# Reordering the first layer's GLU, query/key and gate groups, the pace of the convolution's taps, and the split of q and k, in a hybrid conformer and attention trunk

## The chip, the cores and the metric

The kernel runs on one core of a Trainium2 chip. The metric is device time in microseconds (us) of one execution; "the time before" is the median of three runs. In the profile PE is TensorE (PEld its weight loads), DVE is VectorE, ACT is ScalarE, POOL is GpSimd and SP is SyncE, whose queue issues most of the DMAs.

## What is computed

Two layers over 256 latent tokens (a grid of 4 rows of 64) and 256 context tokens, 1024 channels wide. The second layer (the last) carries only the latent stream and takes keys and values of the context. Of the reference, per layer, cut to the part around the change:

```python
h = modulate(rmsnorm(x, norm1_g[l]), sh1, sc1)      # and hc for the context
p = h @ w_in[l]        # columns: a, g (512 each), q, k, v (512 each), gates (2 x 1024)
...
u = a * sigmoid(g)                                   # "gated channels" (GLU)
u = dwconv1d(u, dw, dw_b)                            # 31 taps along the tokens
y_conv = silu(layernorm(u, ln_g, ln_b)) @ w_o
...
q = rope_2d(q, pos_row, pos_col); k = rope_2d(k, pos_row, pos_col)
y_attn = neighbourhood_attention(q, k, v, k_ctx, v_ctx, rpb) @ w_na_out
yc_attn = context_attention(q_c, k_c, v_c) @ w_na_out      # first layer only
...
x = x + g1 * ((sigmoid(gate_c) * y_conv + sigmoid(gate_a) * y_attn) @ w_out[l])
```

A gated FFN with a convolution of width 3 follows in each layer. The modulation (`sh1`, `sc1`, `g1` and three more of 1024 channels each) is a product of the conditioning vectors with `w_ada`. Everything is float32.

## The kernel before

Channels lie on the 128 partitions, tokens in the free dimension: columns 0 to 255 latent, 256 to 511 context, so an operation over both streams is 512 wide. The kernel is written with a tile framework: the Python code traces instructions in an order, and the framework's planner then puts the instructions of each engine in order, by the traced order among those that its cost model holds to be ready. It may bring a later instruction forward. `tc.issue_after(ins)` adds an edge by which the instructions inside it stand behind `ins` on the engine of `ins`. Each engine executes its list in order.

**A matmul in three parts.** Every product is taken with both operands split in a high part and a rest (`hi`, `lo`): `mm3` (L196 to L199) issues hi x hi, hi x lo and lo x hi. A weight unit of 128 x 1024 comes by `raw_unit` through SP (four buffers), ScalarE casts it (L167 or L216), and the rest is made on VectorE (L168) or, for units in `ADDED`, on ScalarE and a GpSimd DMA that adds (L217, L218). `group` (L201) runs the 24 matmuls of one projection tile; over both streams it calls `slot()` after the twelfth and after the last.

**Slots.** `slot()` (L92) advances every side task by one step. In the first layer's attention stage there are two: `conv_run` (L677), which adds `rate[0]` to a debt and traces as many convolution taps as are due, and `att.run()` (L452), which steps the attention.

**Taps.** `glu(j, ...)` (L687) makes the gated channels `u` of channel block j (0 to 3) from two projection groups (`glu_groups`, L701), with a tanh on ScalarE and a product on VectorE (L693), and appends 31 taps of block j to a list of 124 in all. Each tap is one VectorE instruction, 128 x 512 (L671 for the first of a block, L673 for others). `conv_tap` puts a tap behind the instruction in `after[0]`, which is the latest score (L516, L530).

**Pairs.** Attention works on four pairs of heads. `qk(j)` (L843) projects q and k of pair j (a group each, Q and K), loads the pair's bias, turns the latent part by the rotary tables (L859 to L869: product, shuffle, product, sum on VectorE) and splits the result and the context's part, which is not turned, into `hi` (L881, ScalarE) and `lo` (L882, VectorE). The context's part is read straight from PSUM. For k the latent part is written twice, as `[0, KL)` (the right end of each grid row) and `[KX, KN)` (the left end), with the context between them. The first of a pair's two score products reads context and left end, the second right end and context.

**Attention.** `step` (L457) does at most one round of work per slot, and only when enough slots (2 to 4) lie behind the last round: it turns the probabilities of the round before (`turn`, L544, transposes on TensorE and copies on ScalarE L564 or L567), multiplies older ones by the values (L578, L587), and issues the next score product (`products`, L495) with its softmax (`scores`, L507: L516 on VectorE, L519 exponential and L522 scaling on ScalarE, L521 reciprocal on VectorE). Rounds are "LAT" (a pair's latent queries) and "CTX" (the context's, for two pairs together). `ahead(j)` forces the rounds of pair j and of those before it. PSUM has four banks for projections (`main`), two (`sc`) and one (`pt`) for scores and transposes, and one (`po`).

**Order in the first layer.** After the values (`keep_v`, L719, with 16 small DMAs through SP) come pair 0, GLU 1, pair 1, GLU 2, pair 2, GLU 3, pair 3; GLU 0 was made before. Then up to five gate groups (`gate`, L708) while attention is busy. `rate[0]` is 2 up to pair 1, then 3. Next a second memory pool is opened in place of attention's tiles: in it `ada_dots` (L289) loads further modulation weights (`own`) and multiplies them on VectorE (L304), and `layer_norm` (L938) traces the taps that are left, five a slot, sums the blocks (L949 to L951) and takes that sum to TensorE (L955) five slots later. The remaining gates, the branch products (L993, L998 to L1001) and the output projection follow. The second layer has an order of its own (GLU 2, values, pair 0, GLU 3, then a gate ahead of each further pair), 256 columns for q and 512 for k.

## Time and profile before

| what | value |
|---|---|
| median of three runs | 1056.28 us |
| lowest, highest | 1054.83, 1057.64 us |
| the profiled execution | 1054.58 us |
| its span, first to last instruction | 1052.8 us |
| granted TensorE clock, mean | 0.997 |
| matmuls | 6886 |
| HBM read | 187.63 MB |

The span is what the trace covers; the profiled execution's own time includes some 1.8 us around it. Rows of a timeline give start, duration, engine, line, operation, output and inputs, and in brackets the engine's idle time before the instruction with what ended it. Rows of stretches give the stretch, its length, and then for each engine the busy time with the number of instructions; after these the granted clock, the DMA share and GB/s. A matmul's end is modelled, and matmuls overlap, so the distance from one start to the next tells what one costs.

### The profile page before, as it was taken

The numbers are of one execution on the slowest core, as the hardware profiler recorded it, in microseconds if no ns is written. First come the engines' busy times: TensorE is split into PE (matmuls) and PEld (weight loads), VectorE is DVE, ScalarE is ACT, GpSimd is POOL, SyncE is SP. The second block draws the span as 40 slices with busy tenths as digits, with TensorE's granted clock in tenths as the row PEclk, the third lists the DMA queues.
The fourth block names the chain that finished last, engine by engine and source line by source line (L and its number), as shares of the span: only waits on it lengthen the run. The fifth ranks groups of instructions, "written<-read, shape, count | busy, mean of one in ns | idle before, by whom it ended". The sixth has DMA issues, their size and how long they took to land.

```text
span 1052.8 us, 17991 instructions
## 1 busy us (share of the span) xinstructions
PE 1032.4 (98%) x6886; PEld 932.9 (89%) x6886; DVE 893.2 (85%) x1608; ACT 565.6 (54%) x921; POOL 43.7 (4%) x59
## 2 busy tenths in 40 slices
PE   9999999999999999999999999999999999999997
PEld 7787788888889988888888889999889999999996
DVE  6568899999998787878788888799899988988883
ACT  4458768545434644444444223545777666766652
POOL 1111110011000000000000000000000000000000
PEclk9999999999999999999999999999999999999998
DMA  9989674888945345454545887556734485666781
GB/s 374 305 221 229 156 181 121 258 255 236 305 146 177 104 140 160 140 164 143 166 145 160 301 289 249 180 189 209 208 123 135 161 292 176 193 201 199 221 283 57
DMA packets 59511, 209.26 MB, mean 199 GB/s; under 512 B 7201, under 2 KB 7457, under 8 KB 59425
## 3 DMA queue, kind: packets, MB, share of 16 engines
q1 hardware_dynamic: 54384, 190.77, 55.3%
q0 software_dynamic: 4752, 17.30, 8.7%
q8 instruction: 54, 0.88, 0.3%
q14 instruction: 33, 0.26, 0.1%
q10 hardware_dynamic: 288, 0.04, 0.0%
HBM read 187.63 MB, written 1.05 MB: 179 GB/s over the span
## 4 chain that ended last, share of the span: by engine, by line
PE 68%; DVE 17%; ACT 5%; DMA 4%; issue 3%; SPq 1%; DVEq 0%; ACTq 0%
PE main L197 20%; PE main L198 20%; PE main L199 20%; DVE cb L673 6%; PE main L736 4%; DVE wlo L168 3%; DMA raw<-in_wall 2%; DVE t L304 2%; DMA own<-in_wada 1%; SPq L728 1%; PE sc L197 1%; PE sc L199 1%; PE sc L198 1%; DVE qk L882 1%; ACT pp L519 1%
## 5 line engine op out<-in xcount | busy, mean ns | idle before, releaser
L197 PE MATMUL main<-h,whi 128*128 128x256 f32 (+1 forms) x1328 | 433.1, 326 | 1.2 <-DVE qk L882 1.2
L198 PE MATMUL main<-h,whi 128*128 128x256 f32 (+1 forms) x1328 | 430.2, 324 | 0.9 <-DVE h L1001 0.7
L199 PE MATMUL main<-h,wlo 128*128 128x256 f32 (+1 forms) x1328 | 429.9, 324 | 1.2 <-DVE wlo L168 1.1
L167 ACT CAST whi<-raw 128x1024 fp32r<-128x1024 f32 (+1 forms) x211 | 218.3, 1039 | 234.8 <-PE main L198 173.6
L168 DVE TENSOR_TENSOR wlo<-raw,whi 128x1024 fp32r<-128x1024 f32 (+1 forms) x211 | 253.6, 1208 | 67.2 <-ACT whi L167 66.4
L197 PEld LDWEIGHTS main<-h,whi 128*128 128x128 f32 x1328 | 252.8, 190 | 22.0 <-issue 1.3
L199 PEld LDWEIGHTS main<-h,wlo 128*128 128x128 f32 x1328 | 252.5, 190 | 18.5 <-DVE wlo L168 1.8
L198 PEld LDWEIGHTS main<-h,whi 128*128 128x128 f32 x1328 | 252.7, 190 | 18.3 <-DVE h L1001 1.0
L304 DVE CUSTOM_DVE_ANT_0 t<-own,sb,par 128x1024 bf16<-128x1024 f32 x120 | 151.8, 1282 | 6.8 <-DMA own<-in_wada 6.8
L673 DVE SCALAR_TENSOR_TENSOR cb<-u,par,cb 128x512 f32<-128x512 f32 (+1 forms) x240 | 144.7, 620 | 2.8
L198 PE MATMUL main<-fl,whi 128*128 128x256 f32 (+1 forms) x396 | 122.8, 310 | 0.0
L197 PE MATMUL main<-fh,whi 128*128 128x256 f32 (+1 forms) x396 | 122.8, 310 | 0.0
L199 PE MATMUL main<-fh,wlo 128*128 128x256 f32 (+1 forms) x396 | 122.5, 310 | 0.0
L197 PEld LDWEIGHTS main<-fh,whi 128*128 128x128 f32 x396 | 75.6, 191 | 3.8 <-ACT fh L1095 0.2
L198 PEld LDWEIGHTS main<-fl,whi 128*128 128x128 f32 x396 | 75.6, 191 | 3.7 <-DVE fl L1096 0.2
L199 PEld LDWEIGHTS main<-fh,wlo 128*128 128x128 f32 x396 | 75.5, 191 | 3.6
L216 ACT CAST whi<-raw 128x1024 fp32r<-128x1024 f32 x33 | 34.6, 1049 | 36.0 <-PE main L198 30.5
L404 ACT ACTIVATE h<-t,mod 128x256 fp32r<-128x256 f32 x56 | 25.2, 503 | 34.8 <-DVE t L403 34.3
L218 POOL DMA_DIRECT2D wlo<-raw x33 | 28.9, 877 | 258.9 <-ACT wlo L217 107.6
L736 PE MATMUL main<-whi,h 128*128 128x512 f32 x128 | 38.5, 386 | 0.2
L1105 ACT ACTIVATE t<-t 128x512 f32<-128x512 f32 x22 | 13.9, 632 | 41.3 <-DVE t L1074 41.3
L217 ACT ACTIVATE wlo<-whi 128x1024 fp32r<-128x1024 f32 x33 | 35.0, 1061 | 0.5
(214 smaller groups left out, 1268.8 us busy)
## 6 DMA issues: line engine op xcount, KB each, us to landing
raw<-in_wall SPq DMA_DIRECT2D x240, 512.0 KB, 4.3
own<-in_wada SPq DMA_DIRECT2D x72, 512.0 KB, 4.7
wlo<-raw POOLq DMA_DIRECT2D x33, 512.0 KB, 5.4
raw<-in_wada SPq DMA_DIRECT2D x16, 512.0 KB, 5.8
bias<-in_bias_t SPq DMA_DIRECT2D x8, 520.0 KB, 5.3
row<-in_wada SPq DMA_DIRECT2D x8, 512.0 KB, 5.1
sb<-in_crow SPq DMA_DIRECT2D x5, 512.0 KB, 4.8
x<-in_xt SPq DMA_DIRECT2D x4, 512.0 KB, 5.1
```

Source lines behind the costliest of these rows:

```text
L167: act.copy(hi[:, c], r[:, c])
L168: dve.tensor_tensor(lo[:, c], r[:, c], hi[:, c].bitcast(F32), ALU.subtract)
L197: pe.matmul(ps, w[0], order(xh), start=start, stop=False)
L198: pe.matmul(ps, w[0], order(xl), start=False, stop=False)
L199: pe.matmul(ps, w[1], order(xh), start=False, stop=stop)
L216: act.copy(hi, r)
L217: act.mul(lo, hi.bitcast(F32), -1.0)
L218: pool.dma_start(lo, r, accum_op=ALU.add)
L304: dve.tensor_tensor_reduce(tmp().bitcast(BF16), r, v, 1.0, pr(l, BADA + n, 1), ALU.mult, ALU.add, mods[l][:, n, s : s + 1])
L404: high = act.activation(hi[:, c], y[:, c], AF.Identity, bias=b)
L673: dve.scalar_tensor_tensor(cb[j], src, w, cb[j], ALU.mult, ALU.add)
L736: mm = pe.matmul(pv[t], h1[n == 1][k][:, c], runs(w[n == 2][:, b]), start=k + n == 0, stop=k == KD - 1 and n == 2)
```

## The change

In the first layer GLU 1 is traced before pair 0, and GLU j + 1 before pair j for j = 1 and 2; pair 3 is preceded by gate 0 in place of a GLU group. `glu_groups` asks `ahead` for one pair less, so the rounds that it forces stay at the same pair. The convolution's rate is 3 taps a slot, but for the first group of GLU 2 and of GLU 3 (2 taps a slot). Up to eight gate groups, instead of five, may be traced while attention is busy. For pairs 1 to 3 of the first layer `after[0]` is set to the last split of q, and then to that of k, so that taps traced later stand behind it on VectorE. In both layers the split of the context's part is traced before the second product of the rotation instead of after its sum, and the two ends of k change places: the left end first.

```diff
@@ glu_groups
             def glu_groups(j):
+                if not last and j > 1:
+                    rate[0] = 2.0
                 pa = in_group(T_GLU + 2 * (j - 1), ALL)
+                if not last and j > 1:
+                    rate[0] = 3.0
                 pg = in_group(T_GLU + 2 * (j - 1) + 1, ALL)
-                copied = None if last else att.ahead(j - 2)
+                copied = None if last else att.ahead(j - 3)
...
                 conv = conv_run()
-                rate[0] = 3 if last else 2.0
+                rate[0] = 3.0
                 add_side(conv)
 
+                def parts(f, d, src, sc, view=lambda a: a):
+                    hi, lo = (view(f[:, a, d]) for a in range(2))
+                    act.activation(hi, src, AF.Identity, scale=sc)
+                    return dve.scalar_tensor_tensor(lo, src, sc, hi.bitcast(F32), ALU.mult, ALU.subtract)
+
                 def qk(j):
 
                     att.ahead(j - 2)
+                    if not last:
+                        rate[0] = 3.0
...
                         dve.stream_shuffle(part(r2[:, LAT]), lat, SWAP16)
+                        f = eb.tile([P, 2, KN if what else w], F32R, tag="qk"[what], bufs=2, name=nm("qk"))
+                        if ctx_ is not None:
+                            parts(f, KCTX if what else CTX, ctx_, sc)
                         dve.tensor_tensor(r2[:, LAT], r2[:, LAT], rope[:, 1, :], ALU.mult)
...
                         if what == 0:
-                            to = [([f[:, a, LAT] for a in range(2)], rq[:, LAT])]
-                            if T > S:
-                                to.append(([f[:, a, CTX] for a in range(2)], ctx_))
+                            end = parts(f, LAT, rq[:, LAT], sc)
                         else:
                             rv_ = r1[:, LAT].rearrange("p (r c) -> p r c", r=ROWS)
-                            to = [([f[:, a, KCTX] for a in range(2)], ctx_)]
-                            for d, c in ((slice(0, KL), slice(GW - TC, GW)), (slice(KX, KN), slice(0, TC))):
-                                to.append(([f[:, a, d].rearrange("p (c r) -> p r c", r=ROWS) for a in range(2)], rv_[:, :, c]))
-                        for (hi, lo), src in to:
-                            act.activation(hi, src, AF.Identity, scale=sc)
-                            end = dve.scalar_tensor_tensor(lo, src, sc, hi.bitcast(F32), ALU.mult, ALU.subtract)
+                            for d, c in ((slice(KX, KN), slice(0, TC)), (slice(0, KL), slice(GW - TC, GW))):
+                                end = parts(f, d, rv_[:, :, c], sc, lambda a: a.rearrange("p (c r) -> p r c", r=ROWS))
+                        if not last and j:
+                            after[0] = end
                         both.append(f)
                     att.pair(j, *both, bt, end)
+                    rate[0] = 3.0
 
                 if l == 0:
                     for t in range(4):
                         keep_v(t, pv[t])
+                    rate[0] = 3.0
+                    glu_groups(1)
                     qk(0)
                     arun = att.run()
                     add_side(arun)
-                    for j in range(1, 4):
-                        glu_groups(j)
+                    for j in range(1, 3):
+                        glu_groups(j + 1)
                         qk(j)
-                        rate[0] = 3
...
                 if last:
                     add_side(arun)
-                    for j in range(1, 4):
+                for j in range(1 if last else 3, 4):
+                    if True:
                         gate(ea, n)
                         n += 1
                         qk(j)
-                while att.busy() and n < (14 if last else 5):
+                while att.busy() and n < (14 if last else 8):
                     gate(ea, n)
                     n += 1
```

More of the change, by code (lines that the diff above doesn't have):

```diff
@@ L869, in qk @@
                             dve.tensor_tensor(r1[:, LAT], r1[:, LAT], r2[:, LAT], ALU.add)
-                        f = eb.tile([P, 2, KN if what else w], F32R, tag="qk"[what], bufs=2, name=nm("qk"))
                         if what == 0:
-                            to = [([f[:, a, LAT] for a in range(2)], rq[:, LAT])]
-                            if T > S:
-                                to.append(([f[:, a, CTX] for a in range(2)], ctx_))
+                            end = parts(f, LAT, rq[:, LAT], sc)
                         else:
                             rv_ = r1[:, LAT].rearrange("p (r c) -> p r c", r=ROWS)
-                            to = [([f[:, a, KCTX] for a in range(2)], ctx_)]
-                            for d, c in ((slice(0, KL), slice(GW - TC, GW)), (slice(KX, KN), slice(0, TC))):
-                                to.append(([f[:, a, d].rearrange("p (c r) -> p r c", r=ROWS) for a in range(2)], rv_[:, :, c]))
-                        for (hi, lo), src in to:
-                            act.activation(hi, src, AF.Identity, scale=sc)
-                            end = dve.scalar_tensor_tensor(lo, src, sc, hi.bitcast(F32), ALU.mult, ALU.subtract)
+                            for d, c in ((slice(KX, KN), slice(0, TC)), (slice(0, KL), slice(GW - TC, GW))):
+                                end = parts(f, d, rv_[:, :, c], sc, lambda a: a.rearrange("p (c r) -> p r c", r=ROWS))
+                        if not last and j:
+                            after[0] = end
                         both.append(f)
                     att.pair(j, *both, bt, end)
+                    rate[0] = 3.0
                 if l == 0:
```

## The prediction, made before the change was run

> **What bounds the kernel now.** First the head of the page: its span and TensorE's share.
>
> ```profile
> span 1052.8 us, 17991 instructions
> ## 1 busy us (share of the span) xinstructions
> PE 1032.4 (98%) x6886; PEld 932.9 (89%) x6886; DVE 893.2 (85%) x1608; ACT 565.6 (54%) x921; POOL 43.7 (4%) x59
> ```
>
> TensorE (PE) is busy nearly all the time, VectorE (DVE) comes close behind. The change adds and removes no matmul, so it can only win the time in which TensorE waits. How much that is, is asked of the waits of PE, first in the stretch that the edit rewrites (57 to 300 us: first layer from the value projection to the output projection), then in the second layer's attention (700 to 880 us), whose `qk` is edited too. Columns: who waited for whom, us in total, times, longest.
>
> ```profile
> PE sc L495 <- ACT pT L567: 1.7, 1, 1.7
> PE po L955 <- DVE ss L951: 1.0, 1, 1.0
> PE sc L495 <- ACT qk L881: 0.9, 1, 0.9
> PE main L198 <- DVE h L1001: 0.7, 1, 0.7
> PE sc L495 <- DVE qk L882: 0.6, 1, 0.6
> PE pt L495 <- ACT pT L564: 0.3, 1, 0.3
> ```
>
> ```profile
> PE main L197 <- DVE qk L882: 1.2, 2, 0.6
> ```
>
> The first six rows are 5.2 us, with the seventh 6.4: the ceiling of the gain, but for some tenths by which a matmul restarts slowly after a wait. That is 0.6% of the time; about 0.3% (3.2 us) is what a measurement of this kernel can tell from no change. So the answer hangs on which of seven small waits go and which new ones come.
>
> A window of the FFN, in which nothing waits, gives the price of TensorE's work.
>
> ```profile
> 380.00:400.00 20.00, 20.00 (x94) 17.53 (x93) 16.48 (x24) 9.39 (x12) 0.00 (x0) 1.00 0.50 152
> ```
>
> 94 matmuls of 512 columns in 20 us: 0.215 us each, so a projection group of 24 is 5.2 us. [...]
>
> **The two waits for a pair's q and k.** The products of pair 1 wait for its last split (L881 on ScalarE, L882 on VectorE).
>
> ```profile
> 94.79 0.38 PE L199 MATMUL main<-h,wlo 128*128 128x512 f32 x1
> 96.04 0.44 PE L495 MATMUL sc<-qk,qk 64*128 64x416 f32 x2 [0.87 <-ACT qk L881]
> ```
>
> ```profile
> 94.74 1.54 DVE L673 SCALAR_TENSOR_TENSOR cb<-u,par,cb 128x512 f32<-128x512 f32 x2
> 96.20 0.81 DVE L882 SCALAR_TENSOR_TENSOR qk<-t,qk 128x160 fp32r<-128x160 f32 x2
> ```
>
> Due at 95.0 (94.79 and one matmul), the products get the upper part at 96.04 and the lower one behind L882: 0.9 + 0.6 = 1.5 us. Two taps stand ahead of that L882. Edges behind the chain bar the taps traced after it; those traced before it (Q's and K's slots) may still go first. So I count what VectorE must do between two pairs. Stretches run from pair 0's first score to the end of pair 1's split, then to the end of pair 2's and of pair 3's; the fourth row is for later. First VectorE's busy time, then the taps alone (whose fourth stretch is the end of the convolution).
>
> ```profile
> 77.84:97.01 19.17, 15.28 (x40) 1.00 0.86 239
> 97.01:127.04 30.03, 26.04 (x61) 1.00 0.70 161
> 127.04:153.30 26.26, 25.90 (x57) 1.00 0.79 182
> 213.00:292.20 79.20, 73.72 (x117) 1.00 0.87 259
> ```
>
> ```profile
> 77.84:97.01 19.17, 8.33 (x12) 1.00 0.86 239
> 97.01:127.04 30.03, 15.80 (x22) 1.00 0.70 161
> 127.04:153.30 26.26, 18.04 (x26) 1.00 0.79 182
> 186.90:212.97 26.07, 15.01 (x20) 1.00 0.93 283
> ```
>
> ```profile
> 77.01 0.62 PE L495 MATMUL sc<-qk,qk 64*128 64x416 f32 x4
> ```
>
> Pair 1. After the change, four slots of three lie between pair 0's products and pair 1's chain: 12 taps. Today there are four slots of two, but 12 taps ran: the planner lets later ones forward. VectorE's work stays 15.3 us. TensorE gives it 95.0 - 77.0 = 18.0 us, so there is no wait if VectorE idles under 2.7 us. Today it idles 3.9, nearly all here:
>
> ```profile
> 80.60 0.69 DVE L693 SCALAR_TENSOR_TENSOR u<-t,main 128x512 f32<-128x512 f32 x1 [1.55 <-ACT t L691]
> 83.56 0.16 DVE L521 RECIPROCAL ri<-sm 128x1 f32<-128x1 f32 x1 [2.27 <-ACT pp L519]
> ```
>
> ```profile
> ACT whi L216 <- DMA raw<-in_wall: 5.5, 1, 5.5
> ```
>
> ScalarE is late then because weights came late just before (last row, until 77.0 us), and it catches up on their casts ahead of the tanh and the exponentials. With the second GLU group (two groups, 10.4 us) put before pair 0, the same scores come 10.4 us after that crowd. I take 1.15 of the 1.5 us as won; the bounds are 0 (idling stays) and 1.5.
>
> Pair 2. Its products wait 1.7 us.
>
> ```profile
> 125.32 0.81 ACT L881 ACTIVATE qk<-t 128x160 fp32r<-128x160 f32 x2 [1.58 <-DVE t L869]
> 125.91 1.07 ACT L216 CAST whi<-raw 128x1024 fp32r<-128x1024 f32 x1
> 127.02 1.06 ACT L217 ACTIVATE wlo<-whi 128x1024 fp32r<-128x1024 f32 x1
> 127.98 1.05 ACT L567 COPY pT<-sc 128x512 f32<-128x512 f32 x2
> ```
>
> ```profile
> 128.60 0.44 PE L495 MATMUL sc<-qk,qk 64*128 64x416 f32 x1 [1.69 <-ACT pT L567]
> ```
>
> ScalarE waits 1.58 us for pair 2's chain on VectorE, then does two weight casts, and only then empties the bank that the products want. If the chain is earlier by the 1.7 us that pair 1 and one tap fewer give (slots of 2, 2, 3, 3 and four of 3 are 22 taps; L671's and L673's together were 23), the copies follow it, and the wait shrinks as much. I take 1.2 of 1.7 us (bounds 0 and 1.7), since the casts may still stand ahead.
>
> Pair 3. One gate group takes the place of the last GLU group and the gate behind it.
>
> ```profile
> 154.03 0.82 PE L495 MATMUL sc<-qk,qk 64*128 64x416 f32 x6
> ```
>
> TensorE's time from pair 2's products to pair 3's is now 154.0 - 128.6 = 25.4, afterwards a group less: 20.2 us. VectorE had 25.9 us of work with 27 taps (26 and an L671); 18 are left, and the GLU product goes (0.69 in L693's row). In the chain of waits six taps on end take 3.97 us, 0.66 each:
>
> ```profile
> 135.74 3.97 DVE cb L673 x6
> ...
> 186.88 9.53 DMA own<-in_wada
> ```
>
> 25.9 - 9 x 0.66 - 0.7 = 19.3 us against 20.2: it fits with 0.9 us to spare, less than the in-order idling seen above. I charge 0.3 us (bounds 0 and 2). The softmax wait of 0.3 us (L564) I leave.
>
> **The stage behind attention.** By the slot rules (the stated rests of `step`), the last value product comes after gate 6 instead of gate 4, two groups or 10.4 us later, with no more work for TensorE: those gates are only drawn forward, one weight subtraction with them. By then 12 + 12 + 10 + 12 + 10 + 12 + 6 + 12 + 36 = 122 of 124 taps are traced (GLU 1, pair 0, GLU 2, pair 1, GLU 3, pair 2, gate 0, pair 3, gates 1 to 6); today 20 ran after 186.9 us (15.0 us of VectorE) and the sum over the channels (L951) let TensorE wait 1.0 us at 213. Now the sum has five slots with two traced taps ahead, so that wait goes: 1.0, with the slow restart 1.1 us. The price: `own` tiles can be asked for only when attention's tiles are free. That load took 9.53 us, during which today's last taps run; afterwards VectorE may idle there, and the first modulation dot comes some 8 us later (10.4 less the waits won). About 10 of the 20 taps (6.6 us) ran after that first dot and are gone, a subtraction (1.2 us) too: 7.8 us less work in 8 us less time. VectorE's spare in the next stage is 79.20 - 73.72 = 5.5 us. I charge nothing there and leave L1001's 0.7 us; the cover is those 5.5 us.
>
> **Context's part first.** In the second layer the K group's bank in PSUM is read last by the context's lower part, late:
>
> ```profile
> 761.09 0.42 DVE L882 SCALAR_TENSOR_TENSOR qk<-main,qk 128x256 fp32r<-128x256 f32 x1
> ```
>
> ```profile
> 757.17 0.39 ACT L881 ACTIVATE qk<-main 128x256 fp32r<-128x256 f32 x1 [1.29 <-DVE t L860]
> ```
>
> ```profile
> 761.65 0.45 PE L197 MATMUL main<-h,whi 128*128 128x512 f32 x1 [0.55 <-DVE qk L882]
> ```
>
> Its upper part was ready at 757.56, yet it ran 3.5 us later, behind scores and the rotation's sum; TensorE waited for the bank, and once more in the next pair. Traced ahead of the rotation's second product it can run up to that much earlier, where 0.6 us would do. Won: 1.2 and 0.1 of restart, 1.3 us (bounds 0 and 1.5; a planner that keeps its order gives 0). In the first layer no PE row above names that bank: nothing. Exchanging the two ends of K so that the first product's end comes first wins at most one split, 0.4 us of the 0.81, which lies inside the wait already counted.
>
> **Waits added.** The new edges put the convolution's taps, and behind them nothing but later scores, behind a chain that TensorE wants sooner anyway: no cost as long as the taps end before their sum is asked for. Pair 3's bias request on SP waits for pair 2's scores with one group between instead of two; weight requests stand behind it. No PE row above names a weight in the first layer, so it is hidden by the units asked for in advance.
>
> **The sum**, against the profiled execution of 1054.58 us (span 1052.8 and 1.8 around it; 1.70 below the median of three): -1.15 - 1.2 + 0.3 - 1.1 - 1.3 = -4.45. 1054.58 becomes 1050.1; on the median's footing 1056.28 - 4.45 = 1051.8 us.
>
> **Rivals.** *The waits stay* (0.26): VectorE still idles on ScalarE in pair 1's stretch, the taps traced earlier still go first, pairs 1 and 2 keep their waits. Then -1.1 - 1.3 + 0.3 = -2.1: 1054.2. If the planner also keeps its old order in the second layer (the change doing less than it says), 1055.5. For it: the 12 taps that run there now are as many as are traced there later. Against: the crowd on ScalarE is past.
> *All waits go* (0.10): 6.4 and the restarts' 0.3 to 1.4: 7 to 8 us, 1048.8.
> *The dots come late* (0.14), the slow side: the `own` load collides with weights and takes twice 9.53 us. The first dot is then some 17.5 us late, 7.8 of it paid by less work and 5.5 by the spare; 4.2 us remain, and the gates' product chain (L1001) and the second norm wait as long; with pairs 1 and 2 late as now and pair 3's 2 us the sum is 4.2 + 2 - 1.1 - 1.3 = +3.8: 1060.1. It decides once the first dot starts over 20 us after attention's last product. For it: DMA share 0.93 in that stretch already. Against: the load asks for the same bytes beside fewer weight units.
>
> **How the numbers follow.** Forecast 0.50, its own range 1049.5 to 1054 (bounds of pairs 1 and 2 one way or the other); 0.42 of it lies below 1053.1. Faster: 0.42 + 0.10 = 0.52; same: 0.08 + 0.26 = 0.34; slower: 0.14. The range reaches from 1048.0 (nearly all waits gone) to 1058.0 (the waits that stay, and the 1.4 us by which single runs lie above the median, with pair 3's 2 us).
>
> **What would show it.** Right: no PE wait for L881, L882 or L951 between 57 and 300 us, none over 1 us for L567; VectorE no longer out of taps ahead of pair 0's scores; no PE main L197 waiting for L882 in the second layer; the convolution's sum done before the first dot. Wrong: a PE wait on L881 or L882 at pair 3 over 2 us, a wait on L1001 over 2 us, or PE waiting for weights ahead of the seventh group.

## The result and the profile after

| | before | after |
|---|---|---|
| median | 1056.63 us (6 runs, 1054.83 to 1057.64) | 1069.46 us (6 runs, 1066.71 to 1070.84) |
| ratio of the times, 95% interval | | 1.011 (1.0092 to 1.0129) |
| profiled execution | 1054.58 us | 1070.84 us |
| span; granted clock, mean | 1052.8 us; 0.997 | 1069.1 us; 0.992 |

The change costs 1.1%, 12.8 us by the medians. The two profiled executions lie further apart, 16.26 us, since that of after is its longest run and that of before lies 1.7 us under the median in the front table. The head of the page after: the same matmuls, and TensorE "busier" by 8 us than before (1032.4), which is the first hint that matmuls ran more slowly somewhere.

```profile
span 1069.1 us, 17985 instructions
PE 1040.3 (97%) x6886; PEld 937.6 (88%) x6886; DVE 894.8 (84%) x1608; ACT 564.0 (53%) x921; POOL 43.5 (4%) x59
```

TensorE's waits of after between 57 and 300 us (who for whom, total, times, longest):

```profile
PE main L199 <- DMA wlo<-raw: 2.0, 1, 2.0
PE sc L495 <- ACT pT L567: 1.7, 1, 1.7
PE pt L561 <- ACT pp L522: 1.6, 2, 1.2
PE sc L495 <- DVE qk L850: 1.0, 1, 1.0
PE sc L495 <- ACT pT L564: 0.9, 1, 0.9
...
PE sc L495 <- ACT qk L849: 0.2, 1, 0.2
```

The lines have moved with the diff: L881 and L882 are now L849 and L850, L951 is L963, L998 to L1001 are L1010 to L1013. Of the six rows shown for this stretch of before only the wait for the channel sum (L951) has gone for good. The score waits are still there, in part with other owners, the wait for the last branch step (L1001, now L1013) lies behind 300 us, and a wait for a weight has come.

To see where 16.26 us arose I followed the same landmarks (the first or last matmul of a kind) through both traces:

| from, to | longer by, us |
|---|---|
| start to the last value projection | 0.26 |
| attention, up to its last product with the values (a gate group and a half now stands ahead of it: 36 matmuls, 7.76 us; taken off) | 3.66 |
| from there to the first branch product (the 7.76 put back) | -1.10 |
| the two branch products | 5.35 |
| output projection and the norm ahead of the FFN | 1.95 |
| the FFN's first half | 3.40 |
| from there to the second layer's FFN | 0.48 |
| the second layer's FFN, first half | 2.43 |
| the rest | -0.17 |

The 1.95 us of the output projection are mostly waits for the last branch steps: 0.57 us for L1013 and 1.46 for L1012, at 300 and 304 us, where before had one of 0.66.

### The profile page after: what moved, and what is told of

It is laid out like the page before. It is cut to its first block, busy times and chain, and to the rows that moved or that the text cites. A ratio compares the mean times of both kernels' runs of the same rounds, so it can differ in the third digit from the quotient of the medians.

```text
span 1069.1 us, 17985 instructions
## 1 busy us (share of the span) xinstructions
PE 1040.3 (97%) x6886; PEld 937.6 (88%) x6886; DVE 894.8 (84%) x1608; ACT 564.0 (53%) x921; POOL 43.5 (4%) x59
## 4 chain that ended last, share of the span: by engine, by line
PE 69%; DVE 18%; DMA 4%; issue 4%; ACT 3%; SPq 1%; DVEq 0%; POOL 0%; ACTq 0%; POOLq 0%
PE main L199 21%; PE main L197 21%; PE main L198 21%; DVE cb L673 6%; DMA raw<-in_wall 3%; DVE wlo L168 3%; PE main L740 2%; SPq L732 1%; DMA wlo<-raw 1%; DVE t L403 1%; DVE qk L850 1%; DVE t L304 1%; DVE h L405 1%; PE sc L199 1%; PE sc L197 1%
## 5 line engine op out<-in xcount | busy, mean ns | idle before, releaser
L168 DVE TENSOR_TENSOR wlo<-raw,whi 128x1024 fp32r<-128x1024 f32 (+1 forms) x211 | 252.8, 1204 | 69.8 <-ACT whi L167 69.0
L304 DVE CUSTOM_DVE_ANT_0 t<-own,sb,par 128x1024 bf16<-128x1024 f32 x120 | 150.9, 1277 | 10.5 <-DMA own<-in_wada 10.5
L216 ACT CAST whi<-raw 128x1024 fp32r<-128x1024 f32 x33 | 34.6, 1047 | 37.5 <-DMA raw<-in_wall 22.0
L217 ACT ACTIVATE wlo<-whi 128x1024 fp32r<-128x1024 f32 x33 | 34.7, 1057 | 0.5
```

Of the source, the lines that this page charges most:

```text
L168: dve.tensor_tensor(lo[:, c], r[:, c], hi[:, c].bitcast(F32), ALU.subtract)
L216: act.copy(hi, r)
L217: act.mul(lo, hi.bitcast(F32), -1.0)
L304: dve.tensor_tensor_reduce(tmp().bitcast(BF16), r, v, 1.0, pr(l, BADA + n, 1), ALU.mult, ALU.add, mods[l][:, n, s : s + 1])
```

## Where the time went

**VectorE's cover moved away from the place that needed it.** Three stretches behind attention: last value product to first branch product, the branch products, output projection with norm. Columns: stretch, length, then busy time of PE, PEld, DVE, ACT, POOL, the granted clock, DMA share, GB/s. Before:

```profile
185.57:246.40 60.83, 59.86 (x283) 51.59 (x280) 56.22 (x86) 29.90 (x41) 6.41 (x6) 1.00 0.86 259
246.40:287.62 41.22, 41.22 (x193) 36.10 (x191) 39.32 (x63) 18.44 (x21) 4.34 (x5) 1.00 0.95 281
287.62:332.08 44.46, 43.80 (x296) 40.34 (x295) 41.24 (x85) 18.07 (x32) 0.72 (x1) 1.00 0.46 152
```

and after:

```profile
197.25:249.22 51.97, 51.97 (x247) 44.78 (x244) 39.28 (x61) 26.20 (x36) 5.54 (x5) 1.00 0.87 271
249.22:295.79 46.57, 43.70 (x192) 37.03 (x191) 39.19 (x63) 18.99 (x23) 4.33 (x5) 0.96 0.85 248
295.79:342.21 46.42, 44.01 (x297) 40.26 (x296) 43.98 (x88) 17.46 (x29) 0.72 (x1) 1.00 0.46 151
```

In the first stretch VectorE was idle for 60.83 - 56.22 = 4.6 us, now for 51.97 - 39.28 = 12.7. Taps used to run while `own` was loading (21 taps start in that stretch, now 4), and now VectorE has nothing to do until the load lands. First before, then after:

```profile
196.55 1.28 DVE L304 CUSTOM_DVE_ANT_0 t<-own,sb,par 128x1024 bf16<-128x1024 f32 x1 [0.60 <-DMA own<-in_wada]
```

```profile
203.23 0.42 DVE L596 TENSOR_TENSOR ol<-sc,oh 128x256 fp32r<-128x256 f32 x1 [0.44 <-ACT oh L595]
208.54 1.28 DVE L304 CUSTOM_DVE_ANT_0 t<-own,sb,par 128x1024 bf16<-128x1024 f32 x1 [4.89 <-DMA own<-in_wada]
```

The first dot (a modulation product of L304) starts at 208.54 instead of 196.55, and 18 dots instead of 21 run before the branch stage. Those left over meet the norm ahead of the FFN: in the third stretch there are 14 instead of 12 (the rows count a dot and its read, so two for each). L304 in that stretch, before and after:

```profile
287.62:332.08 44.46, 15.29 (x24) 1.00 0.46 152
295.79:342.21 46.42, 17.66 (x28) 1.00 0.46 151
```

On VectorE in after (the last four dots, 1.2 us or more from one start to the next, ahead of the norm's products, L403, that feed the FFN):

```profile
330.68 1.27 DVE L304 CUSTOM_DVE_ANT_0 t<-own,sb,par 128x1024 bf16<-128x1024 f32 x1
...
334.63 1.28 DVE L304 CUSTOM_DVE_ANT_0 t<-own,sb,par 128x1024 bf16<-128x1024 f32 x1
...
337.38 0.48 DVE L403 SCALAR_TENSOR_TENSOR t<-x,gain,po 128x256 f32<-128x256 f32 x1 [0.47 <-PE po L386]
...
340.48 1.22 DVE L168 TENSOR_TENSOR wlo<-raw,whi 128x1024 fp32r<-128x1024 f32 x1
```

**The branch stage waits for ScalarE's order.** Each weight unit there takes a cast (L216), a subtraction (L217) and a GpSimd DMA that adds. ScalarE's list has three casts, each waiting for TensorE to free a buffer, ahead of all three subtractions, so the three DMAs are asked for after 261 us and TensorE meets the first of them unfinished (ScalarE first, then the DMA, then TensorE):

```profile
249.20 1.04 ACT L216 CAST whi<-raw 128x1024 fp32r<-128x1024 f32 x1 [1.54 <-PE main L198]
254.38 1.04 ACT L216 CAST whi<-raw 128x1024 fp32r<-128x1024 f32 x1 [1.25 <-PE main L198]
259.56 1.04 ACT L216 CAST whi<-raw 128x1024 fp32r<-128x1024 f32 x1 [4.13 <-PE main L198]
260.51 2.95 ACT L217 ACTIVATE wlo<-whi 128x1024 fp32r<-128x1024 f32 x3
```

```profile
261.97 7.17 DMA wlo<-raw
```

```profile
269.18 0.48 PE L199 MATMUL main<-oh,wlo 128*128 128x512 f32 x1 [2.00 <-DMA wlo<-raw]
```

In the trace of before casts and subtractions alternate in that stage:

```profile
251.56 1.05 ACT L216 CAST whi<-raw 128x1024 fp32r<-128x1024 f32 x1 [1.41 <-PE main L198]
252.64 1.06 ACT L217 ACTIVATE wlo<-whi 128x1024 fp32r<-128x1024 f32 x1
```

**The clock fell after small waits.** The trace of after has four stretches of 3.41 us at half the granted clock, at 163.9, 269.7, 348.3 and 880.7 us; the trace of before has none ahead of 1045.7 us, where its last matmuls run. The first one, in three rows of stretches:

```profile
155.00:160.00 5.00, 5.00 (x50) 3.93 (x50) 4.44 (x11) 1.02 (x4) 0.89 (x1) 1.00 0.85 139
160.00:163.90 3.90, 2.88 (x21) 1.57 (x17) 3.78 (x6) 3.44 (x9) 0.00 (x0) 1.00 0.76 247
163.90:167.30 3.40, 3.40 (x10) 2.65 (x9) 3.36 (x7) 0.37 (x1) 0.00 (x0) 0.50 0.55 181
```

TensorE had waited only 0.94 us (its row is the fifth of the waits above), and yet the eight matmuls that start from 163.89 to 166.83 us are 0.38 to 0.43 us apart instead of 0.215: 1.7 us lost in the stretch, and in four such stretches 6.8 us. The last row also explains the head of the page: at a granted clock of 0.50 TensorE counts as busy for all of its 3.40 us.

## The experiments

The change has four parts: the order of the groups, the pace of the taps, the edges, and the context's part first. Each was run by itself on the kernel before, and each was undone by itself in the kernel after. All ratios are to the kernel before.

### Each part alone

Order alone:

```diff
-                copied = None if last else att.ahead(j - 2)
+                copied = None if last else att.ahead(j - 3)
...
+                    glu_groups(1)
                     qk(0)
...
-                    for j in range(1, 4):
-                        glu_groups(j)
+                    for j in range(1, 3):
+                        glu_groups(j + 1)
...
-                    for j in range(1, 4):
+                for j in range(1 if last else 3, 4):
...
-                while att.busy() and n < (14 if last else 5):
+                while att.busy() and n < (14 if last else 8):
```

> The kernel before with the new order of the groups alone (GLU one step ahead, gate 0 ahead of pair 3, up to eight gates); taps, edges and the split as before. Theory A: 1065 to 1070 us, all of the loss. If the loss needs the pace or the edges with it: 1060 us or less.

Pace alone:

```diff
-                rate[0] = 3 if last else 2.0
+                rate[0] = 3.0
```

> The kernel before with 3 taps a slot from the first pair on, nothing else. The prediction's view (the wait of 1.0 us for the sum over the channels at 213 us goes as the taps end earlier, pair 1's split waits up to 1 us more): 1055 to 1057 us. Rival (12 taps in front of pair 1's chain delay it, and the clock halves after it): 1058 to 1061 us.

Edges alone (put behind the split in `qk`):

```diff
+                        if not last and j:
+                            after[0] = end
                         both.append(f)
```

> The kernel before with the edges alone (taps traced behind a pair's last split stand behind it). The prediction's view (the edges cost nothing, since TensorE wants the splits sooner anyway, and pairs 1 and 2 wait less): 1054 to 1057 us. Rival (in the old order the taps barred from moving forward leave VectorE idle ahead of the splits, and run later, towards the sum over the channels): 1058 to 1061 us, with a longer wait for the sum.

Context's part first alone, with the exchanged ends of k; its diff is that of the change in `qk` without `rate` and `after`:

> The kernel before with one part of the change alone: the context's part of q and k split ahead of the rotation's second product, and the two ends of k exchanged, in both layers. Prediction's step: 1.3 us faster, the two waits of a projection group for L882 in the second layer gone (1055.3 us). Rival (the earlier split disturbs the order on VectorE and ScalarE, as the second layer of the changed kernel took 2.9 us longer): 2 to 4 us slower, with new waits of the score products for the copies of the probabilities in the second layer.

| part alone | median, us | ratio, 95% interval |
|---|---|---|
| order | 1064.56 | 1.0067 (1.0047 to 1.0088) |
| pace | 1058.05 | 1.0012 (1.0003 to 1.0021) |
| edges | 1058.58 | 1.0022 (1.0010 to 1.0034) |
| context's part first | 1057.86 | 1.0013 (0.9997 to 1.0029) |

No part wins, and the last one's interval holds 1. 0.67 + 0.12 + 0.22 + 0.13 = 1.14%, beside 1.10% for the whole: the sizes add up, and the order has over half of them. The places don't add up. With the order alone attention itself is 1.0 us shorter, less the group and a half (the trace's first part, ahead of any edit, is 1.3 us longer), and neither of pair 1's two waits is left: what the prediction said of pair 1 holds for this part alone. Nearly the whole loss, 8.6 us, arises where the FFN starts: six dots run at 321.4 to 329.0 us ahead of the norm, the weight subtractions come behind it, and TensorE stands still for one of them:

```profile
340.19 0.58 PE L199 MATMUL sc<-h,wlo 128*128 128x256 f32 x1 [5.39 <-DVE wlo L168]
```

The pace alone makes pair 1's wait longer, with 6.8 us of half clock behind it (a granted clock of 0.75 from 95 to 100 us and of 0.57 from 100 to 105), and the sum's wait (L951) goes as predicted. First TensorE, then VectorE's list ahead of that pair's split: taps stand between the steps of the rotation.

```profile
97.94 0.71 PE L495 MATMUL sc<-qk,qk 64*128 64x416 f32 x2 [2.79 <-ACT qk L881]
```

```profile
95.99 0.74 DVE L673 SCALAR_TENSOR_TENSOR cb<-u,par,cb 128x512 f32<-128x512 f32 x1
96.66 0.42 DVE L869 TENSOR_TENSOR t<-t,t 128x256 f32<-128x256 f32 x1
96.99 0.42 DVE L882 SCALAR_TENSOR_TENSOR qk<-main,qk 128x256 fp32r<-128x256 f32 x1
97.33 0.74 DVE L673 SCALAR_TENSOR_TENSOR cb<-u,par,cb 128x512 f32<-128x512 f32 x1
97.98 0.81 DVE L882 SCALAR_TENSOR_TENSOR qk<-t,qk 128x160 fp32r<-128x160 f32 x2
```

The edges alone shorten the waits of pair 1 (1.07 for 0.87 + 0.58) and pair 2 (1.16 for 1.69), and bring new ones on the scaled probabilities (L522, 1.31, 0.28 and 0.24) and ahead of pair 3's scores (L564, 0.94); up to the first branch product this trace is 2.8 us longer. The time is the rival's, but not by its mechanism: the wait for the sum got shorter, 0.30 for 0.97 us.

### Each part undone

Back to the old order, in the kernel after (the first diff reversed):

> The changed kernel with the old order of the groups (GLU j after pair 0 and between the pairs, at most five gates while attention runs); the pace of three, the edges and the context's part first stay. Theory A (the order of the groups carries the loss): 1055 to 1059 us, near the kernel before. If pace and edges were to blame instead: 1065 us or more.

Back to the old pace: the lines that set `rate` are those of before.

> The changed kernel with the old pace of taps (2 a slot up to pair 1, then 3). Theory A (dots late through the order of the groups): no gain, 1068 to 1073 us, since attention ends as late and more taps are left for the stage behind it. Theory C (three taps a slot crowd VectorE ahead of the pairs' chains): the attention stage gets back its 3.7 us, 1065 us or less.

Without the edges:

```diff
-                        if not last and j:
-                            after[0] = end
```

> The changed kernel without the edges that put taps behind the chains of pairs 1 to 3. Theory A (the loss comes from the order of the groups, through the modulation dots that start 12 us later): 1069 us, no change beyond 2 us. Theory B (edges leave VectorE without taps to fill its gaps in the attention stage, where the change lost 3.7 us): 3 to 4 us faster, 1065 to 1066 us.

Without context's part first, the split being that of before:

> The changed kernel without the context's part first (and without the exchange of k's ends). If that part costs what the second layer lost (2.9 us), this is near 1066 us; if it gains as predicted, near 1071 us; the first layer keeps its 13 us of loss in both cases.

| undone | median, us | ratio, 95% interval |
|---|---|---|
| order | 1060.82 | 1.0029 (1.0014 to 1.0044) |
| pace | 1069.45 | 1.0112 (1.0079 to 1.0145) |
| edges | 1066.15 | 1.0093 (1.0062 to 1.0124) |
| context's part first | 1068.39 | 1.0106 (1.0074 to 1.0139) |

Only the order, undone, gives back much, 8.6 us of the 12.8; the other three intervals overlap that of the change. So from both sides it is the order. The 3.3 us by which the median falls without the edges are the forecast of theory B there, but not clear of the noise: four of the five runs lie at 1066 us, the profiled one at 1071.53. And the old pace gives nothing back in sum, not because it does nothing: in its trace pair 1's two waits are gone, while the FFN's first half, late by 3.4 us in the change, is late by 8.6.

### Behind attention: whose wait is it?

ScalarE's cast of a branch unit put behind the subtraction of the unit before it:

```diff
     def wadded(l, u):
...
-        act.copy(hi, r)
-        act.mul(lo, hi.bitcast(F32), -1.0)
+        with tc.issue_after(lastlo[0].ins) if lastlo[0] and u >= U_NA else ExitStack():
+            act.copy(hi, r)
+        low_ = act.mul(lo, hi.bitcast(F32), -1.0)
+        lastlo[0] = low_ if u >= U_NA else None
```

> The changed kernel, with one edge: in the branch stage ScalarE's cast (L216) of a weight unit stands behind the subtraction (L217) of the unit before it. Theory A (TensorE's wait of 2.0 us for a GpSimd weight there comes from ScalarE's list, which has three casts ahead of three subtractions): that wait and the two of 0.6 us behind it go, and the half-rate stretch of the clock at 348 us with them; the branch stage is 3 to 5 us shorter, the whole 1064 to 1067 us. Rival B (the dots on VectorE, 12 us late, make the branch stage late): the wait only changes its name, the branch stage stays within 1 us, the whole 1068 to 1071 us.

1063.67 us, ratio 1.0063 (1.0043 to 1.0084), 5.8 us less than the change. The branch stage, first without and then with the norm behind it, as its trace has it (after: 46.57 and 46.42 long):

```profile
249.33:291.95 42.62, 41.76 (x192) 35.94 (x191) 40.72 (x66) 19.35 (x23) 4.33 (x5) 1.00 0.92 277
291.95:336.63 44.68, 43.73 (x296) 40.37 (x295) 42.24 (x85) 17.49 (x29) 0.72 (x1) 1.00 0.47 150
```

The weight wait is gone, and no half clock falls into these stretches: 3.9 and 1.7 us back. The FFN's start still loses 3.4 us, with a stretch at half clock at 343 us that theory A wanted gone (the mean granted clock of that execution is 0.994, that of before 0.997). Theory A holds for the branch stage.

Next the dots, traced faster so that none is left over for the norm:

```diff
-                    pace[0] = 1.0 if last else 1.2
+                    pace[0] = 1.0 if last else 1.6
...
-                    pace[0] = 0.7
+                    pace[0] = 1.0
```

> The changed kernel, with the modulation dots of the first layer's gate and branch stages traced faster (1.6 in place of 1.2 dots a slot, then 1.0 in place of 0.7), so that none is left over ahead of the norm before the FFN. Theory A (the FFN's start is late because dots left over are forced ahead of its norm and weight subtractions): the FFN's start loses 3 to 4 us less, the whole 1065 to 1067 us. Rival B (VectorE has no room for them anywhere: the same work crowds the gates and the branch instead): the branch stage or the gates take over the loss, the whole 1068 to 1072 us.

1067.46 us, ratio 1.0099 (1.0069 to 1.0129). The FFN's first half is no longer late (0.03 us against 3.40), but the stage of the branch products has become 8.8 us longer than before, and TensorE waits there for VectorE's gate step (L1005, L993 of before). Stretch of the branch products, and the waits from 197 to 305 us (that of the second row stands at 219.1 us, in a gate group):

```profile
252.04:302.08 50.04, 45.32 (x192) 37.80 (x191) 47.47 (x81) 19.46 (x24) 4.33 (x5) 0.93 0.83 247
```

```profile
PE main L197 <- DVE g L1005: 4.6, 2, 2.3
PE main L199 <- DMA wlo<-raw: 1.9, 1, 1.9
```

The time lies between the two ranges, but this is rival B in its mechanism: the dots find no free place, they only choose whom to delay. Both edits together:

> The changed kernel with both edits, the edge on ScalarE's casts in the branch stage and the faster dots. If the two sites lose independently of each other, the gains add: 1060 to 1063 us. If both are one lack of VectorE's time, the two together give no more than the better one alone, 1065 to 1068 us.

1067.91 us, ratio 1.0103 (1.0070 to 1.0136): nothing adds; the waits for VectorE's gate step (5.0 us in three) stand where the weight wait stood. And the faster dots with the order alone:

> The kernel before with the new order of the groups alone, and the faster dots. The order alone cost 7 us, 8.6 us of it at the start of the FFN. Theory A (dots left over, forced ahead of the norm there): that loss goes, 1056 to 1059 us. Rival B (VectorE's lack of time): another place takes it over, 1062 to 1066 us.

1060.43 us, ratio 1.0027 (1.0012 to 1.0042). The order's 8.6 us at the FFN are gone, 5 us come back in the branch stage (waits of 2.2 us for L995 and 1.9 us for a subtraction L217): between its two theories.

Now with less work for the dots. In the kernel after the context stream's dots of the first layer's modulation tiles 16 to 39 take 128 of 1024 elements, so this kernel leaves out part of that product:

```diff
+                c = slice(0, P) if l == 0 and n < 40 and s == 1 else slice(0, UW)
                 dve.tensor_tensor_reduce(
-                    tmp().bitcast(BF16), r, v, 1.0, pr(l, BADA + n, 1), ...
+                    tmp().bitcast(BF16)[:, c], r[:, c], v[:, c], 1.0, pr(l, BADA + n, 1), ...
```

> The changed kernel with the modulation products of the first layer's stage behind attention shortened for the context stream, to 128 of 1024 elements (the products of 24 tiles for that stream are left incomplete; loads, slots and order stay). It takes some 26 us of VectorE's time out of the stage. Theory A, with VectorE as what the stage lacks: the waits at the branch products, the output projection and the FFN's start (8 to 10 us together) go, 1058 to 1061 us; the attention stage keeps its 3.7 us. Rival (the weights come late through the DMA queues, whatever VectorE does): 1066 us or more.

1065.14 us, ratio 1.0077 (1.0053 to 1.0100). The FFN's first half is 0.3 us late instead of 3.4: the dots on VectorE are the cause of that part. The branch products lose nothing either. The planner has put ScalarE's list in another order there (two casts ahead of two subtractions, then in turn), which fits ScalarE's list as their cause, but VectorE had less to do there too, so this run doesn't tell the two apart. But the wait of 2.0 us for a GpSimd weight has moved forward to a gate group (218.1 us), and three of 2.5 us in all for VectorE's and ScalarE's last branch steps (L1012, L1013 of after) stand in the output projection, each place with half clock behind it: matmuls stand 0.42 to 0.43 us apart from 218.87 to 221.43 us, and again from 303.83 to 307.24. So of the 8.75 us that the two stages had lost (5.35 + 3.40) only 4.3 come back. With the edge on ScalarE added:

> The changed kernel with the edge on ScalarE's casts in the branch stage, and with the context stream's dots of the first layer's modulation tiles 16 to 39 cut to 128 of 1024 elements (part of the sum is left out). Alone the edge gave 5.8 us back and the cut 4.3. Theory A (two sites behind attention, each with a cause of its own, ScalarE's list and VectorE's left-over dots, and what remains is attention's own 3 to 4 us): the gains add, 1058 to 1061 us. Rival B (both only move one lack of VectorE's time about): no more than the better one, 1063 to 1065 us. Theory A': if the rest is only the clock's half-rate stretches, 1056 to 1057 us.

1064.37 us (four runs, 1060.83 to 1066.26), ratio 1.0079 (1.0059 to 1.0099). By its interval the gains don't add, which speaks for rival B, though its shortest run, the profiled one, would fit theory A. That trace, too, has the weight wait in the gate group (1.6 us at 218.1) and waits of 2.5 us for the last branch steps. So the edge had nothing to mend that the cut had not already put in order, and what each cause would give on its own footing stays open.

In the kernel before, the dots alone were traced four slots later:

```diff
+        for _ in range(4 if l == 0 and tiles[0] == 16 else 0):
+            yield
```

> The kernel before with one thing changed: the modulation products behind the first layer's attention, and their loads, begin four slots (two projection groups, 10.4 us) later; the rest of the order is that of the kernel before. Theory A: it shows the loss of the changed kernel behind attention, 5 to 10 us (1061 to 1066 us), with waits at the branch products and the FFN's start. If the start of the dots does not matter: within 2 us of the kernel before.

1059.31 us, ratio 1.0023 (1.0007 to 1.0038). The planner put the first dot at 195.8 us, where it was, and the branch products take 41.22 us as before: tracing the dots later doesn't bring that loss. But 14 dots are left for the stretch of the output projection and the norm (L304 is L306 in this kernel), and the FFN's first half is 3.4 us late, with the same four waits as in after (0.6 us for a subtraction L168, three of 0.2 to 0.4) and a stretch at half clock (mean granted clock 0.995, for 0.997 in before). Those 14 dots:

```profile
286.30:331.68 45.38, 17.66 (x28) 1.00 0.46 144
```

Over all the traces with dots of full length, that loss goes by the number left for this stretch:

| dots there | FFN's first half later by, us | traces |
|---|---|---|
| 12 or fewer | under 0.1, either way | before and eight others, the three with faster dots among them |
| 14 | 3.4 | after; after without the edges, without context's part first, and with ScalarE's edge; before with the dots four slots later |
| 16 | 8.6 to 9.2 | the order alone; after with the old pace, and with the taps in the GLU groups (below) |

So it is the number of dots left over that costs there, and not the hour of the first dot.

### The taps out of the chain

If taps between the steps of the rotation make q and k late, the same taps should do less harm in the GLU groups. In the kernel before:

```diff
                     for j in range(1, 4):
+                        rate[0] = 3.0 if j == 1 else 4.0
                         glu_groups(j)
+                        rate[0] = 1.0 if j == 1 else 2.0
                         qk(j)
```

> The kernel before with the same number of taps per pair, put where no chain runs: 3 (pair 1) or 4 (pairs 2 and 3) a slot in the GLU groups and 1 or 2 in those of q and k. Theory A (a pair's q and k are late because a tap stands between the steps of the rotation on VectorE): pair 1's two waits, 1.45 us, fall below 0.6 us, pair 2's 1.7 us shrinks, the whole 1054 to 1056 us. Rival B (VectorE's total work or ScalarE's casts set the time, or the planner puts the taps back): the waits stay, 1056 to 1058 us.

and in the kernel after (4 a slot in the GLU groups, 1 in the groups of q and k of pairs 1 to 3):

> The changed kernel with 4 taps a slot in the second and third GLU group pairs and 1 in the groups of q and k of pairs 1 to 3 (20 instead of 22 in between). Theory A (taps between the chain's steps): the waits for the split of pair 1 (1.3 us) go, attention ends 1 to 3 us earlier, the whole 1066 to 1068 us. Rival B: the waits stay or take another name, 1068 to 1072 us. In neither is the loss behind attention paid back.

The first: 1054.92 us, ratio 0.9994 (0.9974 to 1.0014), no difference that can be told. Pair 2's wait shrinks from 1.69 to 0.5, pair 1's grows to 2.6 + 0.5: half of theory A. The second: 1065.17 us, ratio 1.0090 (1.0076 to 1.0104), 4.3 us under the change. All waits of pairs 1 and 2 for a split (L849, L850) and for the transposed copies (L567) are gone from its trace, but the room goes to waits for the probabilities, with 6.8 us of half clock behind them (the mean granted clock of that execution is 0.990):

```profile
PE pt L561 <- ACT pp L522: 2.1, 3, 1.5
PE sc L561 <- ACT pp L522: 1.9, 1, 1.9
```

So attention ends only 1.2 us earlier: theory A's mechanism, and rival B's "another name". Nor are the 4.3 us attention's: the branch products get 4.0 us back, the FFN's first half loses 5.8 more (16 dots, and 5.38 us of waiting for a subtraction L168), and the second layer's FFN is 2.6 us shorter. No version ran that beats the kernel before beyond its interval.

## Why the prediction was wrong

The sum said -4.45 us; the medians say +12.8. Step by step:

- **The step that failed most: "I charge nothing there" (the stage behind attention).** Measured in the profiles: 5.35 + 1.95 + 3.40 = 10.7 us. Its cover was "VectorE's spare in the next stage ... 5.5 us", a sum over a stretch. The sum was right to a microsecond (behind the first branch product there were 41.22 - 39.32 + 44.46 - 41.24 = 5.1 us, and three dots of 1.27 us, by the 15.29 us of twelve above, are 3.8), and it didn't help: in the trace of after the left-over dots stand in one place of VectorE's list, ahead of the norm on which the FFN waits (the last four start at 330.68 to 334.63 us, the norm's first product at 337.38). The dots cut short show that part (3.4 to 0.3 us), and so do the numbers of dots left there (12, 14 and 16). "7.8 us less work in 8 us less time" overlooked that the taps filled the time in which `own` loads: VectorE's idle time rose from 4.6 to 12.7 us. The branch products' part is ScalarE's order, shown by the edge there (3.9 of 5.35 us back): a re-sorting by the planner that the prediction has no term for. Why the planner put the casts so is not shown.
- **Pair 1, -1.15 predicted, -0.17 measured** (0.24 + 1.04 for 0.87 + 0.58). The prediction counted 12 taps between pair 0's scores and pair 1's split, 15.3 us of work, and "no wait if VectorE idles under 2.7 us". Now it idles 0.7 us there, so that condition was met, but it has 19.0 us of work, 17 taps in it, and the wait stays:

```profile
87.60:107.30 19.70, 18.43 (x112) 15.29 (x111) 19.01 (x46) 17.26 (x32) 3.46 (x4) 1.00 0.90 229
```

  These are no taps drawn forward: at the end of that split 46 have run, just the 12 + 12 + 10 + 12 that were traced by then. The "four slots" were the slip: 72 matmuls, three groups, run between the two pairs' products, pair 1's two and one of GLU 2, so six slots lie there; of two taps each they give the 12 of before, of three each 18. These taps stand between the steps of the chain (from 97 to 107 us, as in the rows of the pace alone). The reason given for the gain was right: with the order alone, and in the kernel after with the old pace, both waits are gone. The pace of three, part of the same change, brought them back.
- **Pair 2, -1.2 predicted, 0 measured** (1.72 for 1.69). Nothing of pair 1's time was won to pass on, and behind pair 1 a wait of 1.19 + 0.39 us for L522 came, where 0.25 had been: +1.3.
- **Pair 3, +0.3 predicted, +2.6 measured:** a wait of 0.94 us for the copies L564 ahead of its first scores, where there was none, and 1.7 for the half clock behind it. (The 0.3 us wait on L564 that was "left" is another, behind pair 1, and it stayed.)
- **The channel sum, -1.1 predicted, -1.10 measured** from the last value product to the first branch product. Right, in mechanism and size.
- **Context's part first, -1.3 predicted, about 0 measured.** The two waits of the main products for L882 in the second layer are gone, as the list of signs wanted. But from the value projection to the branches that layer is 0.46 us longer, because two score products now wait for the copies behind the transposes, which took 0.2 us before (waits from 700 to 900 us, after):

```profile
PE main L199 <- DVE wlo L168: 2.8, 3, 1.3
PE sc L495 <- ACT pT L564: 1.4, 2, 0.7
```

  Alone, it changed that stretch by -0.08 us. The mechanism was right, the gain wasn't TensorE's to keep: the wait took another name. Of the first row 1.34 + 0.54 us lie in the second layer's FFN, which is 2.43 us longer with the half-clock stretch behind them at 880.7; why these subtractions came later has no cause shown.
- **The clock.** No term of the sum had it. 6.8 us in the profiled execution of after, none in that of before ahead of its end.
- **The first dot, 8 us later predicted, 12.0 measured** (208.54 for 196.55): attention's last value product comes 11.7 us later. Only one and a half gate groups moved ahead of it, 7.76 us where the prediction had two and 10.4, but attention grew by 3.66 us (0.26 arose before it), where it was to shrink by 2.05.
- **Of the signs listed,** three came true: VectorE is no longer idle ahead of pair 0's scores, the second layer's main products don't wait for L882, and the channel sum (201.77 us) is done before the first dot. The waits on the splits and on L567 stayed, and none of the three signs against it came: the loss arose at places that the list did not name.

The rival on the slow side pointed at the right place and sign. Its mechanism was not this one: the first dot started 208.54 - 197.25 = 11.3 us after the last value product, under its 20 us, since `own`, asked for at 200.86 us, took 7.7 us at most and not twice 9.53. Two more dots ahead of the norm suffice, even with the first dot on time, as the dots traced four slots later show. What was weighed least was that each of four edits re-sorts every engine's list: the waits behind attention that decided are waits of an order, not of an amount.

## What to carry to other kernels

Filler work belongs where an engine would otherwise wait for a load (behind attention VectorE idled 12.7 us instead of 4.6 once the taps had been drawn forward): before drawing it forward, look at what stands idle in its old place. A spare of so many microseconds over a stage is no cover for work that stands in one place of an engine's list (here 5.1 us of spare for 3.8 us of dots, and the FFN's first half came 3.40 us later); ask which instruction it will stand ahead of. And where an automatic planner re-sorts the lists after each edit, run the parts by themselves first: here none of four parts won, and one of them had over half of the loss. When work is left over for a place, count it: here the number of dots left told the loss behind them in every trace with dots of full length.

## What the runs showed of the hardware

The half-clock stretches were not expected. In the trace of after the four of them are 3.41 us long each, and from one start to the next (163.9, 269.7, 348.3 and 880.7 us) it is 31, 23 and 156 times as long. Longer ones ran elsewhere: 6.8 us with the pace alone, and in the kernel with both edits matmuls stand 0.42 to 0.59 us apart, but for a further wait between them, from 266.10 to 274.25 us. Those of after follow waits of 0.94, 2.00, 1.21 (three) and 1.88 us (two). Not every such wait is followed by one: that of 1.72 us in after, at 140.3 us, wasn't (the granted clock is 1.00 from 139.4 to 146.2 us), nor was this one of 1.69 us in the trace of before:

```profile
126.90:128.60 1.70, 0.02 (x2) 0.00 (x0) 1.63 (x4) 1.67 (x4) 0.12 (x1) 1.00 0.86 251
128.60:132.00 3.40, 3.35 (x20) 2.64 (x21) 3.33 (x7) 1.91 (x5) 0.74 (x1) 1.00 0.92 231
```

Why half clock follows one wait and not another, no run here shows: none moved a wait and left the rest as it was. What was measured is the price: at 0.50 of the clock a stretch of 3.41 us loses 1.7 us of TensorE's time.
